# A depthwise convolution in a two-block transformer: seven of its 31 taps on ScalarE with accumulating DMAs, and its layer norm's statistics summed before their matmuls

## The chip, the cores and the metric

One core of one Trainium2 chip. The time is the device time of one execution in microseconds, and less is better. 256 tokens of width 2048 go through two transformer blocks; about 500 MB of fp32 weights are read once from HBM.

## What is computed

Block one: attention of three branches beside a conformer convolution, then an output projection and a feed-forward layer; block two is another transformer block. The change touches only the convolution branch of block one:

```python
def conformer_conv(h2, conv_w, conv_b, ln_g, ln_b):
    a, gate = jnp.split(h2, 2, axis=-1)
    u = a * jax.nn.sigmoid(gate)
    u = causal_depthwise_conv(u, conv_w, conv_b)     # 31 taps, 1024 channels, 256 tokens
    u = layer_norm(u, ln_g, ln_b)                    # over the 1024 channels
    return jax.nn.silu(u)
...
    attn = nsa_attention(q, kv, gates, ...)
    conv = conformer_conv(conv_in, ...)
    x = x + jnp.concatenate([attn, conv], axis=-1) @ w_out
```

Tap k multiplies the channel's tokens by one weight and adds them, shifted by s = 30 - k tokens. The layer norm takes mean and variance of each token over all 1024 channels.

## The kernel before

**Weights.** They come as items of 512 KB (`raw`, four buffers, loaded by SP's queue). `split_upto` (line 272) makes of each a rounded copy `hi` on ScalarE (line 281) and the rest `lo` on VectorE (line 282), with four buffers of each, three items ahead of the one that TensorE works on. `run_items` (line 288) does an item in two halves of six products `acc` of 512 columns (`hi` and `lo` with the high part of the activations, `hi` with the low part), twelve in all, and calls `pump` (line 242) after each half.

**Order.** The groups of block one run as `ORDER` says: convolution input quarters c0, c1, c2, the gates g, q0, the compressed branch cmp, c3, the windowed and selected branches' keys win and slc, q1, then the output projection: oc (convolution rows), oa and ob. Everything that isn't weights stands in pipes, lists of closures; `pump` takes steps from them at the rates of `RATES`. Within an engine instructions run in the order in which they were issued.

**The convolution.** Channels lie on the partitions, tokens in the free dimension; a quarter q is two tiles of 128 channels x 256 tokens, kept as one 128x512 tile. `conv_in(q)` (line 493) makes `u` from two projections and puts 31 steps into the pipe `conv`, one for each tap. `conv_tap` (line 517) does both halves of a tap: the first tap (k = 30) on ScalarE with the bias (line 523), the other 30 on VectorE, one multiply-add each into `y` (line 526), 240 in all. After the fourth quarter `conv_norm` (line 529) follows in the same pipe: `mean` multiplies each of the eight tiles by a constant matrix `avg` (8 matmuls), `center` subtracts the mean on VectorE (line 539) and squares on ScalarE (`sqc`, line 541), `var` does 16 matmuls of one column, `rs` and `rs2` make the reciprocal root (`lnv`, `lnd`, `lnr`), and `scale`, `silu` and `low` make `th`, `sh` and `sl`, the activations of the group oc. That group can't start before them; its item asks the pipe for each tile (`mixT`).

**Attention beside it.** The same stretch of the program holds the scores `s`, maxima (line 796) and exponentials (line 802) of the attention pipe, and the copies `kx` (lines 738 and 739) of the transposed keys. POOL issues the loads of bias rows M from a DRAM table gsc, which is itself written by four DMAs of 768 KB from POOL, the small weights w1 and w, and lq.

Of the kernel before, what the change touches and what calls it, by code (L numbers as in the profile page):

```python
# [19 lines left out]
AF = mybir.ActivationFunctionType  # L20
# [16 lines left out]
NRAW = 4  # L37
LN_DVE = 0
ORDER = ["c0", "c1", "c2", "g", "q0", "cmp", "c3", "win", "slc", "q1", "oc", "oa", "ob"]
RATES = {"c1": {"conv": 1}, "win": {"attn": 0.25}, "q1": {"attn": 0.34, "conv": 1.5},  # L40
         "oc": {"attn": 0.5, "conv": 2}, "oa": {"attn": 1}}


# [80 lines left out]
def body(tc, A, out, stop=None, dbg=None):  # L124
# [26 lines left out]
    def U(s="u", dt=F32):  # L151
        return big.tile([P, 512], dt, name=nm(s), tag="U", bufs=NU)

    def two(t):
        return t.rearrange("p (a b) -> p a b", a=2)
# [4 lines left out]
    def bank(s="bg"):  # L160
        return psB.tile([P, 512], F32, name=nm(s), tag="bg")

    def mm(o, l, r, start=False, stop=False):
        pe.matmul(o, l, r, start=start, stop=stop, skip_group_check=True)  # L164
# [171 lines left out]
    def col(name, i):  # L336
        c = offs[name] + i
        return cols[:, c:c + 1]
# [147 lines left out]
    w_in = w2d("w_in")  # L486


    us, ys = {}, {}
    conv, attn = Pipe(), Pipe()  # L490
    mixT = Acts(lambda kt: conv if kt >= 8 else attn)

    def conv_in(q):

        def post(acc):
            s, u = U("sig"), U("ut")
            uu = [two(u)[:, 0], two(u)[:, 1]]
            for t in range(2):
                act.activation(two(s)[:, t], acc[t][:, :T], AF.Sigmoid, scale=rstd[:, t:t + 1])
                dve.scalar_tensor_tensor(uu[t], acc[t][:, T:], rstd[:, t:t + 1], two(s)[:, t],  # L500
                                         op0=ALU.mult, op1=ALU.mult)

            def f():
                us[q], ys[q] = U("u"), U("y")
                turn_plain(us[q], uu, 0)
                for k in range(30, -1, -1):
                    conv.push(lambda k=k: conv_tap(q, k))
                if q == 3:
                    conv_norm()
            urgent.push(None)  # L510
            urgent.push(f)
        return post

    def conv_group(q):
        group(w_in, None, 512, allk, xT, conv_in(q), parts=[(3632 + q * T, T), (2608 + q * T, T)])

    def conv_tap(q, k):
        u2, y2 = two(us[q]), two(ys[q])
        for kk in range(2):
            f = 2 * q + kk  # L520
            w = col("conv_w", k * 8 + f)
            if k == 30:
                act.activation(y2[:, kk], u2[:, kk], AF.Identity, scale=w, bias=col("conv_b", f))
            else:
                s = 30 - k
                dve.scalar_tensor_tensor(y2[:, kk, s:], u2[:, kk, :T - s], w, y2[:, kk, s:],  # L526
                                         op0=ALU.mult, op1=ALU.add)

    def conv_norm():
        st = {}  # L530

        def mean():
            b = st["m"] = bank("mean")
            for f in range(8):
                mm(b[:, :T], avg, two(ys[f // 2])[:, f % 2], start=f == 0, stop=f == 7)

        def center(q):
            mb = st["m"][:, :T].unsqueeze(1).broadcast_to([P, 2, T])
            dve.tensor_tensor(two(ys[q]), two(ys[q]), mb, op=ALU.subtract)
            s = st[q] = U("sqc")  # L540
            act.activation(s, ys[q], AF.Square)

        def var():

            b = st["v"] = bank("var")
            for t in range(2):
                for f in range(8):
                    mm(b[:, t:t + 1], two(st[f // 2])[:, f % 2, t * P:(t + 1) * P], avg[:, 0:1],
                       start=f == t == 0, stop=f == 7)

        half_gb = keep.tile([P, 16], F32, name="half_gb")

        def rs():
            c = offs["conv_ln_g"]
            dve.tensor_scalar(half_gb, cols[:, c:c + 16], 0.5, None, op0=ALU.mult)
            v = small("lnv")
            dve.tensor_scalar(v[:, :2], st.pop("v")[:, :2], EPS, None, op0=ALU.add)
            newton_rstd(v[:, 2:4], v[:, :2], 2)
            d = st["d"] = U("lnd")
            for t in range(2):  # L560
                dve.tensor_scalar(d[:, t * P:(t + 1) * P], ident, v[:, 2 + t:3 + t], 1024.0,
                                  op0=ALU.mult, op1=ALU.mult)

        def rs2():

            b = bank("lnr")
            mm(b[:, :T], avg, st.pop("d")[:, :T], start=True, stop=True)
            r = U("lnr")
            act.copy(r[:, :T], b[:, :T])
            st["r"] = r[:, :T]  # L570

        def scale(q, kk):
            y = two(ys[q])[:, kk]
            dve.tensor_tensor(y, y, st["r"], op=ALU.mult)

            if kk == 0:
                st[q] = U("th")
            f = 2 * q + kk
            g, b = half_gb[:, f:f + 1], half_gb[:, 8 + f:9 + f]
            act.activation(two(st[q])[:, kk], y, AF.Tanh, scale=g, bias=b)  # L580
            if LN_DVE:
                dve.tensor_scalar(y, y, g, b, op0=ALU.mult, op1=ALU.add)
            else:
                act.activation(y, y, AF.Identity, scale=g, bias=b)

        def silu(q):
            y = ys[q]
            dve.scalar_tensor_tensor(y, st.pop(q), 1.0, y, op0=ALU.add, op1=ALU.mult)
            hi = st["hi", q] = U("sh", F32R)
            act.copy(hi, y)  # L590

        def low(q):
            hi, lo = st["hi", q], U("sl", F32R)
            dve.tensor_tensor(lo, ys[q], hi.bitcast(F32), op=ALU.subtract)  # L594
            for kk in range(2):
                mixT.put(8 + 2 * q + kk, two(hi)[:, kk], two(lo)[:, kk])

        for f in (mean, None):
            conv.push(f)
        for q in range(4):  # L600
            conv.push(lambda q=q: center(q))
        for f in (None, var, rs, None, rs2):
            conv.push(f)
        for q in range(4):
            conv.push(lambda q=q: scale(q, 0))
            conv.push(lambda q=q: scale(q, 1), None, lambda q=q: silu(q), None, lambda q=q: low(q))
# [40 lines left out]
    def post_cmp(acc):  # L647
# [24 lines left out]
        def hidden(i):  # L672
            def f():
                b = st[("b", i)] = bank("hid")
                o = b[0:64, :60]
                for lp in range(16):
                    e_, m = divmod(lp, 8)
                    xv = st[i][e_].rearrange("p (h n b) -> p h n b", h=4, b=8)
                    w = w1t[i][e_].rearrange("p (l c) -> p l c", l=8)[:, m]
                    mm(o, w, xv[:, :, e_:e_ + 15, m], start=lp == 0, stop=lp == 15)  # L680
            return f

        def silu():
# [921 lines left out]
```

## Time and profile before

| | us |
|---|---|
| median of 3 runs (lowest, highest) | 2830.05 (2829.97, 2831.06) |
| the profiled execution | 2829.45 |
| its span in the trace | 2827.5 |
| TensorE busy | 2793.4 |
| VectorE busy | 1631.5 |
| ScalarE busy | 1423.6 |

The mean granted clock of TensorE is 0.996 of full speed. The chain of work that ended last lies on TensorE for 96% of the span. A busy time is that of the profiled execution alone; the time of an execution is a little longer than the span of its instructions.

### The profile page before, as it was taken

The numbers are of one execution on the slowest core, as the hardware profiler recorded it, in microseconds if no ns is written. First come the engines' busy times: TensorE is split into PE (matmuls) and PEld (weight loads), VectorE is DVE, ScalarE is ACT, GpSimd is POOL, SyncE is SP. The second block draws the span as 40 slices with busy tenths as digits, with TensorE's granted clock in tenths as the row PEclk, the third lists the DMA queues.
The fourth block names the chain that finished last, engine by engine and source line by source line (L and its number), as shares of the span: only waits on it lengthen the run. The fifth ranks groups of instructions, "written<-read, shape, count | busy, mean of one in ns | idle before, by whom it ended". The sixth has DMA issues, their size and how long they took to land.

```text
span 2827.5 us, 34906 instructions
## 1 busy us (share of the span) xinstructions
PE 2793.4 (99%) x13031; PEld 2314.5 (82%) x13031; DVE 1631.5 (58%) x2472; ACT 1423.6 (50%) x2072; POOL 36.6 (1%) x73
## 2 busy tenths in 40 slices
PE   8998999999999999999999999999999999999998
PEld 7886778888888888889888888888888888888887
DVE  6887765656666554565554545555555455454444
ACT  5456565555555444566544555554454444444443
POOL 1200000000000000000000000000000000000000
PEclk9999999999999999999999999999999999999999
DMA  7853345666556666654566555665566666666664
GB/s 232 236 165 119 116 136 184 187 186 186 180 180 195 198 197 193 179 173 129 170 197 193 172 165 173 179 197 187 183 189 187 192 187 192 187 187 196 197 197 160
DMA packets 279579, 513.01 MB, mean 181 GB/s; under 512 B 21223, under 2 KB 46739, under 8 KB 279409
## 3 DMA queue, kind: packets, MB, share of 16 engines
q1 hardware_dynamic: 272256, 502.86, 58.4%
q0 software_dynamic: 4624, 7.13, 0.9%
q8 instruction: 102, 1.67, 0.2%
q10 hardware_dynamic: 2528, 0.79, 0.1%
q14 instruction: 69, 0.56, 0.1%
HBM read 505.45 MB, written 5.24 MB: 181 GB/s over the span
## 4 chain that ended last, share of the span: by engine, by line
PE 96%; DVE 1%; ACT 1%; issue 1%; DMA 0%; SPq 0%; DVEq 0%; ACTq 0%
PE acc L164 90%; PE tr L391 2%; PE ms L164 1%; PE o L164 0%; DMA raw<-in_w_in 0%; PE ds L164 0%; PE mo L164 0%; PE do L164 0%; DVE lo L282 0%; ACT hi L281 0%; ACT p L802 0%; PE hid L164 0%; PE s L164 0%; PE pt L807 0%; DVE y L526 0%
## 5 line engine op out<-in xcount | busy, mean ns | idle before, releaser
L282 DVE TENSOR_TENSOR lo<-raw,hi 128x1024 fp32r<-128x1024 f32 (+3 forms) x956 | 1153.3, 1211 | 1013.7 <-ACT hi L281 993.1
L281 ACT CAST hi<-raw 128x1024 fp32r<-128x1024 f32 (+3 forms) x956 | 989.8, 1040 | 879.3 <-PE acc L164 821.2
L164 PE MATMUL acc<-hi,xh 128*128 128x512 f32 (+2 forms) x3200 | 1261.2, 394 | 2.8 <-ACT xh L405 2.8
L164 PE MATMUL acc<-hi,xl 128*128 128x512 f32 (+2 forms) x3200 | 1241.8, 388 | 0.5 <-DVE xl L407 0.5
L164 PE MATMUL acc<-lo,xh 128*128 128x512 f32 (+2 forms) x3200 | 1240.0, 388 | 0.0
L164 PEld LDWEIGHTS acc<-hi,xl 128*128 128x128 f32 x3200 | 601.7, 188 | 123.7 <-DVE xl L407 1.0
L164 PEld LDWEIGHTS acc<-hi,xh 128*128 128x128 f32 x3200 | 602.2, 188 | 118.4 <-ACT xh L405 3.0
L164 PEld LDWEIGHTS acc<-lo,xh 128*128 128x128 f32 x3200 | 602.8, 188 | 115.9 <-DVE lo L282 0.5
L164 PE MATMUL acc<-hi,sh 128*128 128x512 f32 x480 | 192.1, 400 | 10.7 <-ACT sh L590 10.7
L164 PE MATMUL acc<-hi,sl 128*128 128x512 f32 x480 | 187.7, 391 | 0.0
L164 PE MATMUL acc<-lo,sh 128*128 128x512 f32 x480 | 187.6, 391 | 0.0
L164 PEld LDWEIGHTS acc<-hi,sh 128*128 128x128 f32 x480 | 90.6, 189 | 29.4 <-ACT sh L590 11.1
L164 PEld LDWEIGHTS acc<-hi,sl 128*128 128x128 f32 x480 | 90.5, 188 | 19.6 <-DVE sl L594 0.2
L164 PEld LDWEIGHTS acc<-lo,sh 128*128 128x128 f32 x480 | 90.7, 189 | 17.6
L526 DVE SCALAR_TENSOR_TENSOR y<-u,cols,y 128x255 f32<-128x255 f32 (+14 forms) x240 | 96.3, 464 | 0.0
L1043 DVE SCALAR_TENSOR_TENSOR yf<-tr,cols,yf 128x254 f32<-128x254 f32 (+1 forms) x176 | 72.6, 475 | 29.3 <-ACT yf L1038 29.3
L1038 ACT ACTIVATE yf<-tr,cols 128x256 f32<-128x256 f32 x88 | 44.8, 560 | 33.7 <-PE tr L391 33.7
L164 PE MATMUL acc<-hi,ymh 128*128 128x512 f32 x128 | 49.8, 389 | 0.0
L164 PE MATMUL acc<-lo,ymh 128*128 128x512 f32 x128 | 49.8, 389 | 0.0
L164 PE MATMUL acc<-hi,yml 128*128 128x512 f32 x128 | 49.8, 389 | 0.0
L428 ACT ACTIVATE e<-acc,rstd 128x512 f32<-128x512 f32 x54 | 37.0, 690 | 25.2 <-PE acc L164 25.2
L434 ACT ACTIVATE junk<-xs 128x512 f32<-128x512 f32 x48 | 30.0, 629 | 35.8 <-DVE xs L442 14.3
(314 smaller groups left out, 1373.5 us busy)
## 6 DMA issues: line engine op xcount, KB each, us to landing
raw<-in_w_in SPq DMA_DIRECT2D x216, 512.0 KB, 3.7
raw<-in_w_up SPq DMA_DIRECT2D x176, 512.0 KB, 3.8
raw<-in_w_down SPq DMA_DIRECT2D x88, 512.0 KB, 4.4
raw<-in_w_ffn_gate SPq DMA_DIRECT2D x88, 512.0 KB, 4.3
raw<-in_w_ffn_up SPq DMA_DIRECT2D x88, 512.0 KB, 3.8
raw<-in_w_ffn_down SPq DMA_DIRECT2D x88, 512.0 KB, 4.3
raw<-in_w_out SPq DMA_DIRECT2D x64, 512.0 KB, 3.7
raw<-in_w_in SPq DMA_DIRECT2D x64, 256.0 KB, 3.4
```

Source lines behind the costliest of these rows:

```text
L164: pe.matmul(o, l, r, start=start, stop=stop, skip_group_check=True)
L281: act.copy(it.hi[:, c], it.raw[:, c])
L282: dve.tensor_tensor(it.lo[:, c], it.raw[:, c], it.hi[:, c].bitcast(F32), op=ALU.subtract)
L391: pe.transpose(b[:, kk * T + t * P: kk * T + (t + 1) * P], src[t][:, c:c + P], ident)
L428: act.activation(u[:, :n], acc[t][:, :n], AF.Copy, scale=scale[:, t:t + 1])
L434: act.activation(j[:, :n], src, AF.Square, accum_out=acc)
L526: dve.scalar_tensor_tensor(y2[:, kk, s:], u2[:, kk, :T - s], w, y2[:, kk, s:], op0=ALU.mult, op1=ALU.add)
L1038: act.activation(y2[:, kk], t2[:, kk], AF.Identity, scale=c(2), bias=col("ffn_conv_b", f))
L1043: dve.scalar_tensor_tensor(y2[:, kk, s:], t2[:, kk, :T - s], col("ffn_conv_w", k * 88 + f), y2[:, kk, s:], op0=ALU.mult, op1=ALU.add)
```

## The change

Of the 31 taps of a quarter, the seven with shift s = 3, 7, 11, 15, 19, 23 and 27 leave VectorE. `conv_product` multiplies on ScalarE: for s = 3 straight into a new tile `z` (POOL clears its first three columns), for the six others into a tile `pr`, which one step of the pipe later a DMA from POOL's software queue adds to `z` (`conv_gather`, 24 in all, some 250 KB each). A gather waits for its product and for the gather before it, both on `z`. After the last tap `conv_join` adds `z` to `y`, and `conv_sum` adds the quarters up in `csum`. `mean` then takes 2 matmuls; the centers stand two to a step, their squares are summed on VectorE one after another, and `var` takes 4 matmuls. The pipe's rate in the group c1 goes from 1 to 0.85, and the compressed branch's `hidden` takes three more steps of the pipe at each of its calls.

```diff
-RATES = {"c1": {"conv": 1}, ...
+RATES = {"c1": {"conv": 0.85}, ...
...
                 for k in range(30, -1, -1):
-                    conv.push(lambda k=k: conv_tap(q, k))
+                    if (30 - k) % 4 == 3:
+                        continue
+                    if (29 - k) % 4 == 1 and k > 1:
+                        conv.push(lambda k=k: (conv_tap(q, k), conv_product(q, k - 1)),
+                                  lambda k=k: conv_gather(q, k - 1))
+                    else:
+                        conv.push(lambda k=k: conv_tap(q, k))
+                conv.push(lambda: conv_join(q))
+                if q:
+                    conv.push(lambda: conv_sum(q))
...
+    def conv_product(q, k):
+        s = 30 - k
+        if s == 3:
+            z = zs[q]
+            pool_e.memset(two(z)[:, :, :s], 0.0)
+        else:
+            z = prods[q, k] = U("pr")
+        for kk in range(2):
+            act.activation(two(z)[:, kk, s:], two(us[q])[:, kk, :T - s], AF.Copy,
+                           scale=col("conv_w", k * 8 + 2 * q + kk))
+
+    def conv_gather(q, k):
+        s = 30 - k
+        if s > 3:
+            pool_e.dma_start(two(zs[q])[:, :, s:], two(prods.pop((q, k)))[:, :, s:],
+                             accum_op=ALU.add)
+
+    def conv_join(q):
+        dve.tensor_tensor(ys[q], ys[q], zs[q], op=ALU.add)
+
+    def conv_sum(q):
+        if q == 1:
+            csum.append(U("csum"))
+        s = csum[0]
+        dve.tensor_tensor(s, ys[q], s if q > 1 else ys[0], op=ALU.add)
...
         def mean():
-            for f in range(8):
-                mm(b[:, :T], avg, two(ys[f // 2])[:, f % 2], start=f == 0, stop=f == 7)
+            s = two(csum.pop())
+            for kk in range(2):
+                mm(b[:, :T], avg, s[:, kk], start=kk == 0, stop=kk == 1)
...
             act.activation(s, ys[q], AF.Square)
+            if q:
+                p = st[q - 1]
+                dve.tensor_tensor(s, s, p, op=ALU.add)
...
         def var():
+            s = two(st[3])
             for t in range(2):
-                for f in range(8):
-                    mm(b[:, t:t + 1], two(st[f // 2])[:, f % 2, t * P:(t + 1) * P], avg[:, 0:1],
-                       start=f == t == 0, stop=f == 7)
+                for kk in range(2):
+                    mm(b[:, t:t + 1], s[:, kk, t * P:(t + 1) * P], avg[:, 0:1],
+                       start=kk == t == 0, stop=kk == 1)
...
-        for q in range(4):
-            conv.push(lambda q=q: center(q))
+        for q in (0, 2):
+            conv.push(lambda q=q: (center(q), center(q + 1)))
...
+                for _ in range(3):
+                    conv.step()
```

**Where the mean stands on TensorE.** Rows are an instruction's line, operation, out<-in and size; a number behind a name tells one tile from another. Before, the mean (one row for each quarter) stands behind the second head group's scores, in the middle of q1:

```order
L164 MATMUL s_2181<-kx_89,q_1168 128x271
L164 MATMUL s_2182<-kx_89,q_1168 128x271
L164 MATMUL s_2181<-kx_89,q_1168 128x143
L164 MATMUL s_2182<-kx_89,q_1168 128x143
L164 MATMUL mean_2203<-y_509,avg 128x256 x2
L164 MATMUL mean_2203<-y_715,avg 128x256 x2
L164 MATMUL mean_2203<-y_929,avg 128x256 x2
L164 MATMUL mean_2203<-y_1671,avg 128x256 x2
L164 MATMUL acc_2023<-hi_2052,xh_278 128x512
L164 MATMUL acc_2023<-lo_2053,xh_278 128x512
```

In the change it stands ahead of the transposes of the keys `kt` that the first scores need:

```order
L164 MATMUL acc_2110<-lo_2030,xh_128 128x512
L164 MATMUL acc_2110<-hi_2029,xl_129 128x512
L164 MATMUL mean_2125<-csum_1333,avg 128x256 x2
L391 MATMUL tr_2128<-ident,kt_2098 128x128 x4
L164 MATMUL acc_2109<-hi_2049,xh_187 128x512
L164 MATMUL acc_2109<-lo_2050,xh_187 128x512
L164 MATMUL acc_2109<-hi_2049,xl_188 128x512
L164 MATMUL acc_2110<-hi_2049,xh_187 128x512
```

So it moved forward past 42 products, two sets of scores and the transposes, and what stands behind it now includes all of these.

**What VectorE does between mean and var.** Before, the four centers stand apart, with an item's `lo` and the gate operations between them:

```order
L539 TENSOR_TENSOR y_509<-y_509,mean_2203 128x512
L282 TENSOR_TENSOR lo_2222<-raw_2056,hi_2221 128x1024
L539 TENSOR_TENSOR y_715<-y_715,mean_2203 128x512
L850 RECIPROCAL rg_2254<-sm_2185 128x4
L853 TENSOR_TENSOR rg_2254<-rg_2254,gates 128x2
L855 TENSOR_SCALAR p_2183<-p_2183,rg_2254 128x256
L856 TENSOR_SCALAR p_2183<-p_2183,rg_2254 128x128
L853 TENSOR_TENSOR rg_2254<-rg_2254,gates 128x2
L855 TENSOR_SCALAR p_2184<-p_2184,rg_2254 128x256
L856 TENSOR_SCALAR p_2184<-p_2184,rg_2254 128x128
L861 TENSOR_TENSOR pc_2068<-pc_2068,cmx_2069 128x8x15
L539 TENSOR_TENSOR y_929<-y_929,mean_2203 128x512
```

In the change they stand behind the first maxima, in one run with the additions of squares (line 585), each of which needs ScalarE's square of the center before it:

```order
L844 ISA cmx_2154 128x1
L580 TENSOR_TENSOR y_509<-y_509,mean_2125 128x512
L580 TENSOR_TENSOR y_725<-y_725,mean_2125 128x512
L585 TENSOR_TENSOR sqc_2188<-sqc_2188,sqc_2185 128x512
L580 TENSOR_TENSOR y_947<-y_947,mean_2125 128x512
L585 TENSOR_TENSOR sqc_2192<-sqc_2192,sqc_2188 128x512
L580 TENSOR_TENSOR y_1737<-y_1737,mean_2125 128x512
L585 TENSOR_TENSOR sqc_2196<-sqc_2196,sqc_2192 128x512
L282 TENSOR_TENSOR lo_2200<-raw_2053,hi_2199 128x1024
L993 SCALAR_TENSOR_TENSOR lj_2205,le_2206<-lq_1958 128x128 x2
```

The `lo` of the next item (line 282) and the lambda operations (line 993) moved behind the whole run.

**What POOL issues ahead of the last join.** Before, gsc's last write, the loads lq and the first M stand together, early in the program:

```order
L711 MEMSET vcmp_1605 128x512
L711 MEMSET vcmp_1611 128x512
L778 DMA gsc<-gm 512x1x384
L356 DMA lq_1880<-in_lambda_q_2 128x128
L356 DMA lq_1880<-in_lambda_k_2 128x128
...
L791 DMA M_2064<-gsc 128x2x256
L791 DMA M_2066<-gsc 128x2x256
L823 MEMSET pc_2068 128x256
L791 DMA M_2571<-gsc 128x2x256
```

In the change gathers (line 542) stand among them; here those of the first quarter (`z_510`) about gsc's first write, and the last four of the fourth (`z_1738`):

```order
L532 MEMSET z_510 128x2x3
L542 DMA z_510<-pr_613 128x2x249
L542 DMA z_510<-pr_658 128x2x245
L826 DMA gsc<-gm 512x1x384
L542 DMA z_510<-pr_712 128x2x241
...
L542 DMA z_1738<-pr_1915 128x2x241
L356 DMA lq_1958<-in_lambda_q_2 128x128
L356 DMA lq_1958<-in_lambda_k_2 128x128
...
L542 DMA z_1738<-pr_1977 128x2x237
L542 DMA z_1738<-pr_2017 128x2x233
L542 DMA z_1738<-pr_2063 128x2x229
L839 DMA M_2149<-gsc 128x2x256
```

gsc's first write now stands between the second and the third gather of the first quarter; the lq loads moved between the third and the fourth gather of the last, the M loads behind its last.

## Rows read from the trace of the kernel before

**Rows 1.** The page's first part (busy time and share of the span of each engine) and the head of its fourth (the chain that ended last, by engine).

```profile
...
PE 2793.4 (99%) x13031; PEld 2314.5 (82%) x13031; DVE 1631.5 (58%) x2472; ACT 1423.6 (50%) x2072; POOL 36.6 (1%) x73
...
PE 96%; DVE 1%; ACT 1%; issue 1%; DMA 0%; SPq 0%; DVEq 0%; ACTq 0%
...
```

**Rows 2.** Windows: the stretch in us, its length, then for each engine the busy time in it and (x) its instructions: TensorE, its weight loads, VectorE, ScalarE, POOL; then the granted TensorE clock as a share of full speed, the DMA engines' busy share, GB/s.

```profile
...
200.00:220.00 20.00, 20.00 (x95) 16.21 (x94) 19.91 (x38) 10.95 (x16) 0.00 (x0) 1.00 0.71 207
220.00:240.00 20.00, 16.89 (x72) 13.31 (x71) 17.90 (x71) 8.72 (x23) 1.75 (x3) 0.91 0.42 132
240.00:260.00 20.00, 11.41 (x73) 9.53 (x71) 11.59 (x37) 15.08 (x29) 2.26 (x4) 0.88 0.33 103
260.00:280.00 20.00, 17.92 (x94) 13.58 (x94) 13.68 (x40) 15.42 (x32) 1.82 (x3) 0.86 0.26 77
400.00:2827.00 2427.00, 2418.38 (x11142) 2016.74 (x11140) 1322.02 (x1693) 1197.35 (x1627) 4.92 (x16) 1.00 0.60 184
...
```

**Rows 3.** TensorE's waits over the whole span: the waiting instruction, what it waited for, us in all, times, the longest.

```profile
...
PE acc L164 <- ACT sh L590: 10.7, 1, 10.7
...
PE mean L164 <- DVE y L526: 3.1, 1, 3.1
...
```

**Rows 4.** TensorE's timeline: start, time taken, line, operation, out<-in, how many records; in brackets the idle time before and what ended it.

```profile
...
212.05 0.39 PE L164 MATMUL acc<-lo,xh 128*128 128x512 f32 x1
212.28 0.39 PE L164 MATMUL acc<-hi,xl 128*128 128x512 f32 x1
...
215.23 0.60 PE L391 MATMUL tr<-ident,kt 128*128 128x128 f32 x4
...
227.34 2.86 PE L164 MATMUL mean<-y,avg 128*128 128x256 f32 x12
233.30 1.13 PE L164 MATMUL mean<-y,avg 128*128 128x256 f32 x4 [3.11 <-DVE y L526]
...
243.41 3.62 PE L164 MATMUL var<-avg,sqc 128*128 128x1 f32 x32
...
250.82 0.59 PE L164 MATMUL lnr<-lnd,avg 128*128 128x256 f32 x2
262.08 0.79 PE L164 MATMUL acc<-hi,sh 128*128 128x512 f32 x1 [10.67 <-ACT sh L590]
...
263.10 0.63 PE L164 MATMUL acc<-hi,sl 128*128 128x512 f32 x1
263.53 0.63 PE L164 MATMUL acc<-hi,sh 128*128 128x512 f32 x1
...
268.13 0.60 PE L391 MATMUL tr<-ident,e 128*128 128x128 f32 x4
...
```

**Rows 5.** Windows of 5 us, columns as in rows 2.

```profile
...
230.00:235.00 5.00, 1.89 (x8) 1.49 (x8) 5.00 (x10) 0.00 (x0) 0.72 (x1) 0.98 0.32 105
235.00:240.00 5.00, 5.00 (x17) 3.87 (x17) 3.34 (x19) 3.32 (x10) 0.31 (x1) 0.68 0.55 159
260.00:265.00 5.00, 2.92 (x7) 2.29 (x8) 2.80 (x7) 4.90 (x10) 0.00 (x0) 0.50 0.13 48
...
```

**Rows 6.** The page's group of the VectorE taps (count, busy us, mean ns of one, idle before), and the instructions of line 523 with least, median and greatest duration in ns.

```profile
...
L526 DVE SCALAR_TENSOR_TENSOR y<-u,cols,y 128x255 f32<-128x255 f32 (+14 forms) x240 | 96.3, 464 | 0.0
...
L523 ACT ACTIVATE y<-u,cols x8: 587/592/601, 46.3 to 186.5; 128x256 f32<-128x256 f32 x8
...
```

**Rows 7.** VectorE's timeline, columns as in rows 4.

```profile
...
214.18 1.59 DVE L526 SCALAR_TENSOR_TENSOR y<-u,cols,y 128x239 f32<-128x239 f32 x4
215.69 1.22 DVE L282 TENSOR_TENSOR lo<-raw,hi 128x1024 fp32r<-128x1024 f32 x1
...
220.38 0.42 DVE L796 CUSTOM_DVE_ANT_0 p<-s,M 128x256 f32<-128x256 f32 x1
...
221.85 2.32 DVE L526 SCALAR_TENSOR_TENSOR y<-u,cols,y 128x234 f32<-128x234 f32 x6
...
236.13 0.69 DVE L539 TENSOR_TENSOR y<-y,mean 128x512 f32<-128x512 f32 x1
...
```

**Rows 8.** ScalarE's timeline, columns as in rows 4.

```profile
207.26 1.05 ACT L281 CAST hi<-raw 128x1024 fp32r<-128x1024 f32 x1 [1.66 <-PE acc L164]
209.98 1.06 ACT L281 CAST hi<-raw 128x1024 fp32r<-128x1024 f32 x1 [1.67 <-PE acc L164]
...
213.47 1.06 ACT L281 CAST hi<-raw 128x1024 fp32r<-128x1024 f32 x1
215.87 0.58 ACT L738 COPY kx<-tr 64x512 f32<-64x512 f32 x1 [1.33 <-PE tr L391]
...
242.76 1.23 ACT L541 ACTIVATE sqc<-y 128x512 f32<-128x512 f32 x2
...
```

**Rows 9.** DMA issues in four stretches, 60 to 74, 86 to 95, 230 to 240 and 264 to 272 us: out<-in, the issuing queue, how many, KB each, median us from issue to landing.

```profile
...
gsc<-gm POOLq DMA_DIRECT2D x1, 768.0 KB, 12.2
...
M<-gsc POOLq DMA_DIRECT2D x2, 256.0 KB, 14.9
...
M<-gsc POOLq DMA_DIRECT2D x1, 256.0 KB, 4.2
...
M<-gsc POOLq DMA_DIRECT2D x2, 256.0 KB, 3.4
...
```

**Rows 10.** POOL's timeline, columns as in rows 4.

```profile
...
234.14 0.72 POOL L791 DMA_DIRECT2D M<-gsc  x1 [7.26 <-issue]
...
```

More of the change, by code (lines that the diff above doesn't have):

```diff
@@ L39 @@
 ORDER = ["c0", "c1", "c2", "g", "q0", "cmp", "c3", "win", "slc", "q1", "oc", "oa", "ob"]
-RATES = {"c1": {"conv": 1}, "win": {"attn": 0.25}, "q1": {"attn": 0.34, "conv": 1.5},
+RATES = {"c1": {"conv": 0.85}, "win": {"attn": 0.25}, "q1": {"attn": 0.34, "conv": 1.5},
          "oc": {"attn": 0.5, "conv": 2}, "oa": {"attn": 1}}
@@ L486, in body @@
     w_in = w2d("w_in")
-    us, ys = {}, {}
+    us, ys, zs, prods = {}, {}, {}, {}
     conv, attn = Pipe(), Pipe()
@@ L503, in f @@
             def f():
-                us[q], ys[q] = U("u"), U("y")
+                us[q], ys[q], zs[q] = U("u"), U("y"), U("z")
                 turn_plain(us[q], uu, 0)
                 for k in range(30, -1, -1):
-                    conv.push(lambda k=k: conv_tap(q, k))
+                    if (30 - k) % 4 == 3:
[8 more added lines that the diff above has]
+                    conv.push(lambda: conv_sum(q))
                 if q == 3:
@@ L527, in conv_tap @@
                                          op0=ALU.mult, op1=ALU.add)
+    csum = []
+    def conv_sum(q):
[3 more added lines that the diff above has]
+        dve.tensor_tensor(s, ys[q], s if q > 1 else ys[0], op=ALU.add)
     def conv_norm():
```

## The prediction

> **What bounds the kernel now.** I read the page first: TensorE is busy 99% of the span and carries 96% of the chain that ended last, so only time in which TensorE stands still or runs slowly can be won [rows 1]. Then the busy time by 20 us: the reader sees 20.00 of 20 at a clock of 1.00 up to 220 us, then 16.89, 11.41 and 17.92, and after 400 us 2418 of 2427 [rows 2]. All that this change touches lies before 270 us. TensorE's waits name two in that stretch: 10.7 us for the first `sh` of the output projection, 3.1 us for the last tap of the convolution [rows 3]. TensorE's timeline places them: the mean's twelve records at 227.34 and, after the wait, four at 233.30; var's 32 at 243.41; nothing between `lnr` at 250.82 and 262.08 [rows 4]. After both waits the clock falls to its lower level, 1.2 GHz: 0.68 on average in 235 to 240, 0.50 in 260 to 265 [rows 5]; products then start 0.43 us apart, not 0.23 [rows 4], which costs 1.8 us after the first wait and 1.6 after the second (8 to 9 products each). Lost from 212 to 268: 3.1 + 10.7 + 1.8 + 1.6 = **17.2 us**.
>
> **TensorE's own saving.** mean goes from 8 matmuls to 2, var from 16 to 4. Mean's records take 2.86 + 1.13 = 4.0 us, of which three quarters go: 3.0. Var's take 3.6; 2.7 go [rows 4]. Together 5.7 us. With the 17.2 the most that could be won is 22.9 us, if nothing new were waited for.
>
> **Seven taps leave VectorE.** 56 of the 240 taps [rows 6], some 0.375 us each from start to start (four in 1.59, [rows 7]), are 21 us less there; four joins, three sums and three additions of squares at about 0.65 (a 128x512 tensor operation takes 0.69, [rows 7]) put 6.5 back. ScalarE gets 56 products. The nearest row is the first tap, already a ScalarE product from SBUF: 592 ns [rows 6], so some 0.55 us each, 31 us spread over 170. Before 212 us neither is on TensorE's path: TensorE is full there [rows 2], and ScalarE's next copy `hi` waits 1.67 us of each 2.72 us for TensorE to free a buffer [rows 8]; one or two products fit in that. Cost and gain: 0. If that cover is gone, the products show as a late `hi`, at most 1.1 us per item.
>
> **Six gathers per quarter.** Each is a software-queue DMA of about 250 KB that adds `pr` to `z`; it waits for its product and for the gather before it, and POOL waits in order, so M, gsc, w1 and lq loads are queued behind it and it behind them. No row shows an accumulating DMA. The nearest are POOL's 256 KB copies of M: 3.4 and 4.2 us from issue to landing, 14.9 right behind the 768 KB gsc [rows 9]. An accumulation reads its target too, so I bound L, issue to landing, by 3.4 below and by 7 (twice the bare copy) above, and take **4.4**, just above the copy. The Trainium skill ("DMA: Bandwidth & Descriptors", Anatomy of one DMA) gives 2.0 us plus bytes over 436 GB/s, an estimate of 2.6; the copies here are slower, and the sum would be the same by it.
>
> The last quarter decides. Its products stand behind the copies `hi` of the items in order, at about 184, 189.4, 192.2, 197.7, 203.1 and 208.9 (the last behind the `hi` of 207.26, [rows 8]). With L = 5.25 the gathers land at 189.3, 194.7, 199.9, 205.2, 210.4 and 215.7; the join can start, as shown next, at 215.7. So up to 5.25 nothing is late. In the first quarter the third gather stands behind gsc, whose landing takes 12.2 [rows 9]; it is about 8 us late there, and the weights' lookahead of three items (3 x 2.72) covers that at 4.4.
>
> **The chain from 212 to 268.** Here `hi` of q1's fourth lookahead item runs at 213.47 [rows 8]; its `lo` no longer stands behind taps and ends at 215.7 (before: it started at 215.69). Join and sum, 2 x 0.65: `mean` starts at 217.0. It now stands on TensorE ahead of the transposes that were done at 215.23 [rows 4]: a new wait of 1.8 us, and transposes, four copies `kx` (0.6 each), `hi`, `lo` and the maxima (1.47, from 220.38 to 221.85, [rows 7]) all follow it: maxima end at 224.7, before at 221.85.
>
> Then two engines hand over in turn. VectorE: center 0, 1, add, center 2, add, center 3, add; ScalarE: a square after each center, 0.6 [rows 8]. Center 0 ends 225.4, square 1 at 226.7, add 1 at 227.4, center 2 at 228.0, its square 228.6, add 229.3, center 3 at 229.9, square 230.5, add **231.15**. TensorE is at `var` at 225.0: a new wait of 6.2 us. Next `hi`, `lo` (232.6), the lambda and gate operations (235.3), variance to `lnd` 2.0 us as before (247.07 to 249.0): `lnr` at about 238, against 250.82.
>
> So the statistics come 13 us earlier. But the work between them and the transposes of `e` is the same as before, and before it was done while TensorE stood still: ScalarE was busy 15.1 and 15.4 of 20 us in those slices [rows 2]. In order on ScalarE now: `hi`, maxima and four exponentials to 245.1, three tanh pairs (1.12 each) to 248.5, `sh` 249.0, `hi` 250.1 and `lo` 251.2 of oc0, `sl` of the second tile 254.2 (TensorE waits 2.5), `hi` and `lo` of oc1 to 259, the two other `sh`, `hi` and `lo` of oc2 to 265.1, exponentials 267.3, the two `e` at **268.5**. The transposes of `e` then start at 268.6; before, at 268.13 [rows 4]. TensorE stands still some 10 us just ahead of them.
>
> Check by TensorE: 52.9 us before (215.23 to 268.13), less 17.2 and 5.7, is 30; new waits 1.8 + 6.2 + 0.8 + 2.5 + 10 = 21.3; half-clock products between them 2. Sum 53.3, as above.
>
> **Sum.** +0.5 us at the transposes of `e`, and the lower clock after the 10 us wait, 1.6, which before fell ahead of that point: **+2 us**. The profiled execution took 2829.45 (span 2827.5); with the change 2831.5. The median of the runs is 0.6 above it: **2832**. Some forty steps of the chain are added by hand; I give it 4 us to either side, 2828 to 2836. A measurement here tells 0.2%, 5.7 us, from no change: 2824.3 to 2835.7.
>
> **Rivals.** *A, slower: the gathers become the chain.* It decides from L = 5.25 on. At 6 us the last quarter lands at 220.0, 4.3 us late, at 7 at 226, 10.3 late, and all of the chain above moves with it. The first two quarters, with gsc and the w1 loads in the same queue, add up to as much again, since their 8 us of lookahead are used up: 2836 to 2841 at 6, 2842 to 2853 at 7; I price it at **2843**. For it: the 14.9 us behind gsc, a DMA share of 0.71 in 200 to 220 [rows 2] where the M copies saw less. Against: no M copy that stood alone took over 4.2. The Trainium skill ("DMA: Bandwidth & Descriptors", Queues, rings and completion order) has descriptors of one ring start in order, and the 14.9 agrees.
>
> *B, slower: POOL cannot issue beside VectorE.* VectorE is busy 19.91 of 20 us in 200 to 220 [rows 2]; if an issue waited for it, L would grow by a `lo` or a run of taps, 1.2 to 2.3 us, to about 6.2: **2839** by A's steps. Against it: POOL issued M in 0.72 us at 234.14 [rows 10], in a stretch of 5 us in which VectorE was busy all 5.00 [rows 5]. The Trainium skill ("SBUF — State Buffer", SBUF: two separate sides) says that a POOL-issued DMA starves while VectorE runs in a two-port mode, 620 ns growing to 3100; no row here shows it.
>
> *C, faster: the hand-over is shorter than I booked.* From 217 to 268.5 are 51 us, of which ScalarE is busy 36 by my steps; 15 are waits for VectorE. If two thirds of them fall away because operations run beside each other that I put in line, the transposes of `e` come 10 us earlier: **2822**; if all do, 2817; the cap of 22.9 off the median of before gives 2807. A third, 2827, is still the forecast. For it: the statistics are ready 13 us earlier and TensorE has 21 us of slack. Against: both engines work in program order, and every step above waits for the one before.
>
> **How the numbers follow.** Forecast 0.50, A 0.27, B 0.04, C 0.19. Of the forecast 0.04 lie above 2835.7, and of C 0.01 above 2824.3: faster 0.18, same 0.47, slower 0.35. The range leaves out half of C (below 2822) and the part of A with L over 6.5 (above 2848).
>
> **What would show it.** The wait for taps gone, TensorE idle 1 to 3 us ahead of `mean` at about 217, 5 to 8 ahead of `var`, 8 to 11 ahead of the transposes of `e` near 268.6, and mean and var of some 1 us each; gathers landing in under 5.25 us. Wrong, if the gathers take over 5.25 and the join of the last quarter starts after 216, or if the transposes of `e` start before 263 with TensorE hardly waiting.

## The result and the profile after

| | before | with the change |
|---|---|---|
| median of 4 runs, us | 2830.01 | 2854.25 (2852.15 to 2858.40) |
| the profiled execution, us | 2829.45 | 2855.76 |
| its span, us | 2827.5 | 2853.9 |

The change is slower: ratio 1.0086, 95% interval 1.0074 to 1.0098, some 24 us, above the range of 2822 to 2848. The forecast said no change; of its rivals the one that came about is A, the gathers as the chain, and it cost more than priced.

The page of the change, answering to [rows 1]:

```profile
...
PE 2801.0 (98%) x12995; PEld 2316.6 (81%) x12995; DVE 1617.9 (57%) x2426; ACT 1444.5 (51%) x2128; POOL 65.6 (2%) x101
...
PE acc L164 84%; PE tr L391 2%; DMA z<-pr 2%; DMA raw<-in_w_in 1%; PE ms L164 1%; DVE lo L282 1%; ACT hi L281 1%; PE o L164 0%; ACT p L850 0%; PE ds L164 0%; PE mo L164 0%; PE do L164 0%; PE s L164 0%; PE pt L855 0%; PE pt L856 0%
...
```

VectorE lost only 13.6 us of its busy time, ScalarE gained 21, and in the chain a term stands that was not there before: the landing of gathers, 2% of the span by itself. TensorE's waits, against [rows 3]:

```profile
...
PE mean L164 <- DVE csum L567: 9.6, 1, 9.6
PE tr L391 <- ACT e L428: 5.4, 3, 3.8
PE var L164 <- DVE sqc L585: 4.9, 1, 4.9
PE pt L855 <- DVE mx L844: 4.5, 1, 4.5
PE tr L391 <- DVE ut L500: 3.9, 1, 3.9
PE s L164 <- ACT pts L858: 3.5, 1, 3.5
...
```

The 10.7 us for `sh` and the 3.1 for the last tap are gone, as forecast. But the wait ahead of `mean` is 9.6 us, not 1.8, and TensorE now loses time early in the program too. Two of its early windows in the kernel before, columns as in [rows 2]:

```profile
...
100.00:120.00 20.00, 20.00 (x94) 16.57 (x93) 17.20 (x32) 9.28 (x11) 0.00 (x0) 1.00 0.74 218
180.00:200.00 20.00, 20.00 (x92) 16.57 (x91) 19.43 (x38) 12.44 (x18) 0.00 (x0) 1.00 0.69 191
...
```

The same two, and 220 to 240, with the change:

```profile
...
100.00:120.00 20.00, 15.69 (x66) 11.85 (x64) 13.87 (x26) 7.43 (x11) 6.23 (x8) 1.00 0.88 245
180.00:200.00 20.00, 16.10 (x62) 12.73 (x61) 13.98 (x23) 14.29 (x25) 2.93 (x5) 0.83 0.72 205
220.00:240.00 20.00, 10.37 (x44) 8.29 (x43) 10.38 (x18) 5.39 (x10) 4.21 (x5) 0.86 0.77 226
...
```

TensorE loses 4.3 us in 100 to 120 and 3.9 in 180 to 200, where it was full before, and half of 220 to 240, where it lost 3.1 before [rows 2]. VectorE's timeline (start and length in us, line, operation, and in brackets the idle time before it with its releaser) tells of the first and the third place:

```profile
...
86.04 0.81 DVE L557 SCALAR_TENSOR_TENSOR y<-u,cols,y 128x226 f32<-128x226 f32 x2
93.20 0.69 DVE L546 TENSOR_TENSOR y<-y,z 128x512 f32<-128x512 f32 x1 [6.34 <-POOL z L532]
...
237.38 0.69 DVE L546 TENSOR_TENSOR y<-y,z 128x512 f32<-128x512 f32 x1 [7.37 <-DMA z<-pr]
238.11 0.69 DVE L567 TENSOR_TENSOR csum<-y,csum 128x512 f32<-128x512 f32 x1
```

The join of the first quarter keeps VectorE idle for 6.3 us (the bracket names an older event of `z`; the sixth gather was issued at 89.20 and landed at 93.1), that of the last for 7.4. The way from the first join to TensorE leads through a weight load: `lo` of item 30 stands behind it and runs at 93.81 (88.87 before), so the buffer that it frees is loaded at 95.06 and not at 90.11, and ScalarE's `hi` at 105.52 waits 7.75 us for these weights. POOL's timeline, in the same columns, shows why they are late:

```profile
...
60.88 1.62 POOL L826 DMA_DIRECT2D gsc<-gm  x1
66.08 1.20 POOL L542 DMA_DIRECT2D z<-pr  x1 [3.58 <-ACT pr L536]
77.47 1.18 POOL L542 DMA_DIRECT2D z<-pr  x1 [10.19 <-ACT pr L536]
...
168.62 1.18 POOL L542 DMA_DIRECT2D z<-pr  x1 [3.75 <-DMA z<-pr]
169.32 1.00 POOL L735 MEMSET hidv<- 64x512 f32 x1
...
213.67 1.24 POOL L542 DMA_DIRECT2D z<-pr  x1 [0.95 <-issue]
222.79 1.21 POOL L542 DMA_DIRECT2D z<-pr  x1 [7.88 <-DMA z<-pr]
229.23 1.20 POOL L542 DMA_DIRECT2D z<-pr  x1 [5.23 <-DVE y L557]
...
```

The third gather (66.08) stands behind gsc's first write and lands 10.9 us later; the fourth is issued 0.5 us after that (the bracket at 77.47 names the product, which had long been made). So it is nearly everywhere: of the 20 gathers that follow another one of their quarter, 19 are issued 0.5 to 0.6 us after its landing. The fourth of the last quarter (213.67), behind the lq loads, lands after 8.5 us, and POOL waits 7.88 us for it. The landings, in the columns of [rows 9], first of 60 to 80 us, then of 200 to 215:

```profile
...
gsc<-gm POOLq DMA_DIRECT2D x1, 768.0 KB, 13.5
z<-pr POOLq DMA_DIRECT2D x1, 245.0 KB, 5.3
z<-pr POOLq DMA_DIRECT2D x1, 241.0 KB, 10.9
z<-pr POOLq DMA_DIRECT2D x1, 237.0 KB, 5.2
...
z<-pr POOLq DMA_DIRECT2D x1, 241.0 KB, 3.8
z<-pr POOLq DMA_DIRECT2D x1, 237.0 KB, 8.5
lq<-in_lambda_q POOLq DMA_DIRECT2D x2, 64.0 KB, 6.2
...
```

And ScalarE's timeline shows the second place, which no step of the prediction had:

```profile
...
161.16 0.21 ACT L733 ACTIVATE hidk<-hid 64x60 f32<-64x60 f32 x1
170.36 0.53 ACT L739 ACTIVATE hidv<-hid 64x60 f32<-64x60 f32 x4 [8.98 <-POOL hidv L735]
...
180.12 2.13 ACT L763 COPY vcmp<-vc 32x128 f32<-32x128 f32 x8 [4.72 <-POOL vcmp L759]
...
```

The compressed branch's tiles hidv and vcmp are cleared by memsets on POOL. At 169.32 the memset of hidv stands behind a gather that waited for the landing of the one before (POOL's rows above), and ScalarE, with every later `hi` behind it, waits 8.98 and then 4.72 us.

Where the time went is read best from the copy `hi` of each item (counted from 0): its start against the same item's in the kernel before (ScalarE's timelines, us). The labels are those of the experiments below.

| item | before, start | change | e3 | e8 | e12 | e9 | e10 |
|---|---|---|---|---|---|---|---|
| 31 | 91.15 | -1.0 | +0.2 | -1.5 | -0.1 | -1.2 | -1.7 |
| 41 | 120.11 | +7.1 | +0.2 | -1.1 | -0.1 | -1.2 | +7.9 |
| 61 | 185.03 | +13.8 | +0.2 | +9.9 | -0.1 | -1.2 | +15.8 |
| 71 | 213.47 | +13.8 | +0.2 | +9.9 | +3.7 | -0.4 | +13.3 |
| 83 | 283.23 | +26.2 | +3.3 | +22.4 | +16.4 | +11.9 | +16.7 |

(The -1 to -1.7 of the early items is in place before the first gather.) The change loses in three steps: 8.1 us behind the first join, 6.7 about the memsets, 12.3 from the last join on. After the 83rd item nothing more is lost.

### The profile page after: what moved, and what is told of

Same layout as the page of the kernel before. It is cut to its first block, busy times and chain, and to the rows that moved or that the text cites. A ratio compares the mean times of both kernels' runs of the same rounds, so it can differ in the third digit from the quotient of the medians.

```text
span 2853.9 us, 34913 instructions
## 1 busy us (share of the span) xinstructions
PE 2801.0 (98%) x12995; PEld 2316.6 (81%) x12995; DVE 1617.9 (57%) x2426; ACT 1444.5 (51%) x2128; POOL 65.6 (2%) x101
## 4 chain that ended last, share of the span: by engine, by line
PE 89%; DMA 3%; ACT 2%; DVE 2%; issue 1%; POOL 0%; DVEq 0%; SPq 0%; ACTq 0%; POOLq 0%
PE acc L164 84%; PE tr L391 2%; DMA z<-pr 2%; DMA raw<-in_w_in 1%; PE ms L164 1%; DVE lo L282 1%; ACT hi L281 1%; PE o L164 0%; ACT p L850 0%; PE ds L164 0%; PE mo L164 0%; PE do L164 0%; PE s L164 0%; PE pt L855 0%; PE pt L856 0%
## 5 line engine op out<-in xcount | busy, mean ns | idle before, releaser
L557 DVE SCALAR_TENSOR_TENSOR y<-u,cols,y 128x255 f32<-128x255 f32 (+22 forms) x184 | 74.3, 464 | 0.0
```

## The experiments

Theory Q: the gathers, in POOL's queue, cost nearly all of it. Rival S: the statistics' serial chain of center, square and addition does. Each ratio is against runs of the kernel before that were made beside it.

**e3, no gathers.** The edit, in `conv_gather`:

```diff
-            pool_e.dma_start(two(zs[q])[:, :, s:], two(prods.pop((q, k)))[:, :, s:],
-                             accum_op=ALU.add)
+            prods.pop((q, k))
```

> The change without its 24 accumulating DMAs: the products of six of the seven taps are made on ScalarE and left out of the sum; all else stays. Theory Q: 2829 to 2834, the forecast's 2832 with nothing late in the queue: mean at about 217, var's wait some 6 us. Rival S: 2845 or more, unchanged by the DMAs. A third case, ScalarE's products themselves delay hi: over 2836 with ScalarE's hi late by 0.5 us or more in 60 to 210.

Measured 2832.52, ratio 1.0008 (0.9999 to 1.0018): the forecast's number. TensorE's timeline in the stretch that the prediction worked out by hand:

```profile
...
217.36 1.13 PE L164 MATMUL mean<-csum,avg 128*128 128x256 f32 x4 [1.79 <-DVE csum L566]
...
231.71 1.64 PE L164 MATMUL var<-avg,sqc 128*128 128x1 f32 x8 [5.05 <-DVE sqc L584]
...
238.47 0.74 PE L164 MATMUL lnr<-lnd,avg 128*128 128x256 f32 x2
...
254.72 0.92 PE L164 MATMUL s<-kd,q 64*128 64x256 f32 x6 [3.49 <-ACT pts L857]
...
267.36 0.48 PE L854 MATMUL pt<-ident,p 128*128 128x128 f32 x1 [4.51 <-DVE mx L843]
...
269.62 1.47 PE L391 MATMUL tr<-ident,e 128*128 128x128 f32 x4 [1.35 <-ACT e L428]
...
```

`mean` at 217.4 after a wait of 1.79 (forecast 217.0 and 1.8), var at 231.7 after 5.05 (231.2 and 6.2), `lnr` at 238.5 (238), the transposes of `e` at 269.6 (268.6), with 3.49, 4.51 and 1.35 us idle ahead of them in three waits (10). So the gathers cost 22 us and everything else in the change 2.5. As the cause of the 22 us S falls, and so does the third case: ScalarE's products hold back no `hi` for long (items 49 and 50, at 144 and 145, are 0.4 and 0.9 us late, item 51 is 0.2 again).

**e1, sums only.** All taps on VectorE as before, no products, c1's rate 1, no extra steps; csum, paired centers and the sums of squares stay:

```diff
-                    if (29 - k) % 4 == 1 and k > 1:
-                        conv.push(lambda k=k: (conv_tap(q, k), conv_product(q, k - 1)),
-                                  lambda k=k: conv_gather(q, k - 1))
...
-                conv.push(lambda: conv_join(q))
+                    conv.push(lambda k=k: conv_tap(q, k))
```

> Only the sums of the change: all taps as before, no product on ScalarE, no DMA; csum, paired centers, squares summed on VectorE, 2 + 4 matmuls. Theory Q (the gathers in POOL's queue cost nearly all of the 24 us): no loss of that size here, between 2828 and 2838; the taps last as long as before, so the wait ahead of mean stays and the serial centers follow it. Rival S (the statistics' serial chain of center, square and addition costs it): 2845 or more, with the waits ahead of var and of the first sh longer by over 10 us.

Measured 2841.65, ratio 1.0039 (1.0024 to 1.0053): between the two cases, 3.7 above Q's range. So the sums are not free by themselves. TensorE's timeline:

```profile
...
238.67 2.05 PE L164 MATMUL mean<-csum,avg 128*128 128x256 f32 x4 [8.18 <-DVE csum L559]
...
251.37 1.86 PE L164 MATMUL var<-avg,sqc 128*128 128x1 f32 x8 [5.39 <-DVE sqc L577]
...
263.02 1.22 PE L164 MATMUL lnr<-lnd,avg 128*128 128x256 f32 x2 [3.31 <-DVE lnd L598]
273.55 0.80 PE L164 MATMUL acc<-hi,sh 128*128 128x512 f32 x1 [9.30 <-ACT sh L627]
...
```

The taps are as long as before, but two of the three sums stand in the pipe ahead of the last taps: VectorE does two of these (four instructions) at 236.26, behind an item's `lo` and the second maxima, where before all were done ahead of both, at 233.6. The last sum follows. So `mean` waits 8.2 us (3.1 before) and starts at 238.7, and the serial squares and the scaling follow 20 to 25 us later than in e3. The sums cost 12 us where the taps end late, and nothing that e3 shows where they end early.

**e2, products and gathers only.** mean, center and var as in the kernel before; all else as in the change:

```diff
-            s = two(csum.pop())
-            for kk in range(2):
-                mm(b[:, :T], avg, s[:, kk], start=kk == 0, stop=kk == 1)
+            for f in range(8):
+                mm(b[:, :T], avg, two(ys[f // 2])[:, f % 2], start=f == 0, stop=f == 7)
```

> Products and gathers as in the change, mean and var as before (8 and 16 matmuls, single centers, no additions). Theory Q: 2848 to 2856, since the gathers stay; join of the last quarter as late as in the change. Rival S: 2832 to 2838.

Measured 2854.24, ratio 1.0082 (1.0067 to 1.0097): as Q says. With the gathers in, the form of the statistics makes no difference that these runs can tell.

**e6, plain copies.** The accumulation is taken out of the DMA:

```diff
-            pool_e.dma_start(two(zs[q])[:, :, s:], two(prods.pop((q, k)))[:, :, s:],
-                             accum_op=ALU.add)
+            pool_e.dma_start(two(zs[q])[:, :, s:], two(prods.pop((q, k)))[:, :, s:])
```

> The change with its gathers as plain copies, without the accumulation (six of the seven products overwrite one another in z, so they are left out of the sum); every wait and the queue stay. If the accumulation itself makes the landing long: copies of about 250 KB land in 3.4 to 4.2 us as M's did, and the time falls to 2836 to 2846. If queue and company make it (theory Q as I now hold it): alone 3.5 to 5 us, still 8 to 11 beside gsc, w1 and lq, and 2848 to 2855.

Measured 2835.10, ratio 1.0014 (1.0005 to 1.0024), a little under the first case; the ten runs lie between 2832.24 and 2837.34, and the trace is of one of 2832.28. All instructions and waits are those of the change; only the accumulation is gone, and with it 19 us. So theory Q in the form that it then had (queue and company make the landing long, whatever is moved) missed: it needs the accumulation. The group of the gathers' issues in the change (shortest, median and longest in ns, then the first and the last start):

```profile
...
L542 POOL DMA_DIRECT2D z<-pr x24: 1165/1188/1289, 54.2 to 229.2; - x24
...
```

The same group in e6:

```profile
...
L542 POOL DMA_DIRECT2D z<-pr x24: 711/714/738, 54.0 to 210.6; - x24
...
```

And the landings (last column, median us), in the change:

```profile
...
z<-pr POOLq DMA_DIRECT2D x4, 249.0 KB, 6.5
...
z<-pr POOLq DMA_DIRECT2D x4, 233.0 KB, 5.5
...
```

and of the same two sizes in e6:

```profile
...
z<-pr POOLq DMA_DIRECT2D x4, 249.0 KB, 4.7
...
z<-pr POOLq DMA_DIRECT2D x4, 233.0 KB, 3.2
...
```

The record of an issue is 1.19 us long with the accumulation and 0.71 without; but POOL isn't held up longer, since its next instruction starts 0.7 us after the issue in both (168.62 to 169.32 in POOL's rows above; 81.73 to 82.43 in e6). What differs is the landing, 5.5 to 6.5 us against 3.2 to 4.7 in these rows. That doesn't look like 19 us; but the six of a quarter are in series. In the change 18 of the 24 land after 3.7 to 5.9 us, 4.7 in the median; in e6 20 land after 2.5 to 5.0, 4.2 in the median. The next issue comes some 0.55 us later in both: a period of 5.2 us against 4.7, where the prediction's schedule allows 5.25. The others, beside gsc, w1, lq and M, land after 7.5 to 11.0 us (six) and 5.5 to 8.0 (four). The change stood at the point where the chain keeps up, with nothing left for the late ones.

**e7, two chains.** Two tiles `z`, used in turn; shifts 3 and 7 go straight into them, 20 gathers remain, two joins:

```diff
-        if s == 3:
-            z = zs[q]
+        if s in (3, 7):
+            z = zs[q][s == 7]
...
-            pool_e.dma_start(two(zs[q])[:, :, s:], ...
+            pool_e.dma_start(two(zs[q][(s // 4) % 2])[:, :, s:], ...
```

> Two tiles z, taken in turn: shifts 3 and 7 go straight into them, the five gathers of a quarter alternate, so a gather waits for the landing of the one before the last, and 20 gathers remain; the join becomes two additions. Theory Q: POOL no longer stands still for a landing, the gathers behind gsc, w1 and lq overlap, and most of the 22 us go: 2833 to 2842, with DMA waits ahead of the joins under 3 us in all. Rival: the bandwidth of the queue is the limit rather than the wait for each landing; then 2848 to 2856.

Measured 2834.70, ratio 1.0013 (1.0004 to 1.0022). VectorE's waits, in the columns of [rows 3], have one for a landing ahead of a join, where the change had three, of 16.5 us in all:

```profile
...
DVE y L547 <- DMA z<-pr: 0.4, 1, 0.4
...
```

Of the 12 gathers that follow another one into their tile three are issued 0.5 us after its landing (78.43, 81.14 and 153.80), the others over a microsecond after it. They land no sooner (5.6 to 7.3 us in the medians by shift); it is the wait of each for the one before that costs, not the queue's bandwidth. That each quarter also has one gather less may be a part of it; no run has a single chain of five.

**e5, additions on POOL; e11, additions on VectorE.** In place of the DMA:

```diff
+            z = two(zs[q])[:, :, s:]
+            pool_e.tensor_tensor(z, z, two(prods.pop((q, k)))[:, :, s:], op=ALU.add)    # e5
+            dve.tensor_tensor(z, z, two(prods.pop((q, k)))[:, :, s:], op=ALU.add)       # e11
```

> The change with each of the 24 accumulating DMAs replaced by an addition z += pr on POOL itself (tensor_tensor, 128 x 2 x 249 and less): same products, same order on POOL, no transfer to land. Theory Q (the landing of the gathers, 3.7 to 5.6 us alone and 8 to 11 in company, is the chain): an addition under 4 us cannot be late in any quarter, so 2831 to 2836, as without gathers (2832.5). Rival: POOL and VectorE hold one another up; then the taps on VectorE grow above 0.46 us or the additions above 5 us, and the time is 2840 or more.

> The change with each gather replaced by an addition z += pr on VectorE: nothing stands in POOL's queue, VectorE takes 24 x 0.6 = 14 us of its 21 back. Theory Q: 2832 to 2838, the taps of the last quarter ending some 3 us later than without gathers. Rival (VectorE's load of these quarters matters as much as the queue): 2840 or more.

e5: 2844.10, ratio 1.0045 (1.0030 to 1.0060), 8 us above Q's range; e11: 2834.35, ratio 1.0014 (1.0005 to 1.0024), within it. In e5 an addition takes 1.65 us (the middle of the three numbers) and 3.47 at most, so none is late by itself, as the group of POOL's additions shows:

```profile
...
L543 POOL TENSOR_TENSOR z<-z,pr x24: 1215/1645/3468, 54.6 to 216.4; 128x498 f32<-128x498 f32 x4, 128x490 f32<-128x490 f32 x4, 128x482 f32<-128x482 f32 x4, 128x474 f32<-128x474 f32 x4
...
```

What it loses instead it loses on VectorE, as the rival said. The group of the taps in e3 and then in e5, in the columns of [rows 6]:

```profile
...
L556 DVE SCALAR_TENSOR_TENSOR y<-u,cols,y 128x255 f32<-128x255 f32 (+22 forms) x184 | 74.1, 462 | 0.0
...
L557 DVE SCALAR_TENSOR_TENSOR y<-u,cols,y 128x255 f32<-128x255 f32 (+22 forms) x184 | 96.3, 580 | 0.0
...
```

Beside the additions the same 184 taps take 22 us more; 23 of them take over 0.6 us, the median (0.46) doesn't show it. It costs 7.5 us at one place: `lo` of item 42 runs at 126.45 (122.29 in e6), so the weights of item 46 are loaded at 127.69, 1.9 us behind gsc's third write (125.84), and ScalarE's `hi` at 140.60 waits 8.36 us for them. In e6 the same load goes out at 123.55, 3.3 us ahead of the write, and is in time. The last quarter costs 5 us more than in e3 (`mean` waits 4.6 us). e11 puts 24 additions of 0.65 us, 16 us, back on VectorE and costs 2 us over e3.

**e9 and e10, where.** Gathers in the last quarter alone, and in the first three alone:

```diff
-        if s > 3:
+        if s > 3 and q == 3:    # e9
+        if s > 3 and q < 3:     # e10
```

> The change with gathers in the last quarter alone (six DMAs); the products of the other quarters are made and left out of the sum. If the losses add up by place: without gathers 2832.5, and the last quarter's own 9 us (its copies hi fell back 12.3 us in the change, 3.3 without gathers) give 2839 to 2844. If the last quarter is late only because the earlier ones are: 2832 to 2836.

> The complement: gathers in the first three quarters alone (18 DMAs), the last quarter's six products left out of the sum. If the losses add up by place: 2832.5 plus the 8 us up to the 41st item and the 6.7 between the 50th and the 60th, 2845 to 2849. If they are the same backlog, carried to the end: 2836 to 2843.

e9: 2842.39, ratio 1.0044 (1.0027 to 1.0061); e10: 2846.51, ratio 1.0055 (1.0040 to 1.0070). Over e3's 2832.5 that is 9.9 and 14.0; together 2856.4, against the change's 2854.3. Within 2 us, the runs' own spread, the losses add up by place. In the first three quarters there is more than in the last, on which the prediction had put its weight.

**e4, e8 and e12, the first three quarters.** e4 puts the memsets on VectorE:

```diff
-            pool_e.memset(hv[0:64], 0.0)
+            dve.memset(hv[0:64], 0.0)
...
-                pool_e.memset(v, 0.0)
+                dve.memset(v, 0.0)
```

e8 leaves them and moves the joins of the first three quarters ten taps into the next one:

```diff
+                    if q and k == 20:
+                        conv.push(lambda: conv_join(q - 1))
+                        if q > 1:
+                            conv.push(lambda: conv_sum(q - 1))
...
-                conv.push(lambda: conv_join(q))
-                if q:
-                    conv.push(lambda: conv_sum(q))
                 if q == 3:
+                    conv.push(lambda: conv_join(q))
+                    conv.push(lambda: conv_sum(q))
```

e12 is e8 with the memsets still on POOL, but issued ahead of the compressed branch's matmuls (hidv's at 139.4, in e8 at 165.9):

```diff
+                if i == 0:
+                    st["hv"], st["vc"] = U("hidv"), [U("vcmp"), U("vcmp")]
+                    pool_e.memset(st["hv"][0:64], 0.0)
+                    for v in st["vc"]:
+                        pool_e.memset(v, 0.0)
                 av = two(turn4(e, i * T))
```

> The change with the memsets of hidv and vcmp on VectorE rather than on POOL, where they stand behind gathers. In the trace of the change ScalarE waits 9.0 and 4.7 us for them near 170 and 180, and the copies hi fall back by 6.7 us between the 50th and the 60th item. Theory Q, POOL's order part: those two waits go and the time falls by 4 to 7 us, to 2847 to 2850. Rival (the waits are covered, the loss there is the gathers' own chain): less than 2 us.

> The change with the joins of the first three quarters ten taps into the next quarter, rather than right behind the last tap; the last quarter's stays. In the trace of the change VectorE stands 6.3 us ahead of the first join, the copies hi then fall back 8 us between the 31st and the 41st item. Theory Q: those 7 to 8 us go and the last quarter's 9 to 12 stay: 2842 to 2849. Rival (the loss at the 31st to 41st item comes from the weight loads beside gsc and w1, not from the join): 2851 to 2856.

> Late joins (as in the run with late joins alone) and the memsets of hidv and vcmp issued on POOL ahead of the compressed branch's matmuls, so that no gather stands before them; all gathers stay. With late joins alone the copies hi fell back 10 us between the 51st and the 60th item and ScalarE waited 12.1 and 4.9 us for the two memsets. If POOL's order makes that loss: those waits go, and what is left is the last quarter's 9.9 us over 2832.5, so 2840 to 2846. If the gathers' own chain makes it: 2850 to 2856, with VectorE waiting for the landing ahead of the late joins.

e4: 2855.56, ratio 1.0093 (1.0076 to 1.0110); e8: 2855.09, ratio 1.0087 (1.0070 to 1.0104); e12: 2847.01, ratio 1.0063 (1.0046 to 1.0080). By their times e4 and e8 do nothing, as the rivals said. The table tells otherwise for e8: the 8 us up to the 41st item are gone, and between the 51st and the 60th 10 come back. Ten taps later VectorE stands at no join, but the next quarter's first gather now falls right behind gsc's third write (issued at 138.09, 1.2 us behind the write, landed after 17.2 us), the rest of that quarter queue behind it, and ScalarE waits 12.1 us for the memset. In e4 the memset only changed its queue: on VectorE it stands behind the taps that the extra pipe steps bunch up, as VectorE's timeline of e4 shows:

```profile
...
161.38 3.87 DVE L557 SCALAR_TENSOR_TENSOR y<-u,cols,y 128x242 f32<-128x242 f32 x10
...
166.31 0.83 DVE L557 SCALAR_TENSOR_TENSOR y<-u,cols,y 128x235 f32<-128x235 f32 x2
167.19 0.48 DVE L735 MEMSET hidv<- 64x512 f32 x1
```

There ScalarE waits 6.0 and 5.0 us for VectorE. Only e12 takes away both, and then the 61st item is where it was before (table); its ScalarE timeline shows no wait where there were 8.98 us:

```profile
...
155.31 0.21 ACT L740 ACTIVATE hidk<-hid 64x60 f32<-64x60 f32 x1
155.43 0.52 ACT L745 ACTIVATE hidv<-hid 64x60 f32<-64x60 f32 x4
```

Left is the last quarter, 12.7 us from the 71st to the 83rd item (3.1 without gathers), and 3.8 just before, where the first gather again falls behind gsc; so e12 ends 1 us above what was expected. In the first three quarters taking one loss away (e8) let the next one grow in its place, and only both edits together (e12) show what each is worth.

## Why the prediction was wrong

- **The step that failed** is the one that took L = 4.4 us for every gather and said "up to 5.25 nothing is late", and that the first quarter's lookahead covers its gather behind gsc. Measured in the change, 18 of the 24 land in 3.7 to 5.9 us, 4.7 in the median, and the next is issued 0.5 us after the landing (66.08 + 10.9 = 77.0, issue 77.47), which the chain of the prediction left out: some 5.2 in all, the limit itself. The other six, beside gsc, w1, lq and M, take 7.5 to 11 us, beyond its upper bound of 7, two of them in the quarter that was to decide. The prediction had the 12.2 and the 14.9 of [rows 9] and booked such company for one gather of the first quarter only; the three items of lookahead that were to cover it did not, as 8.1 us were lost behind the first join.
- **Rival A** had the mechanism and its point of decision (5.25), but it priced "the first two quarters" at "as much again" as the last and the third at nothing. The first three cost 14.0 us (e10), the last 9.9 (e9). Missing was a consumer: the list of what stands behind a waiting POOL named loads and not the two memsets, for which ScalarE waits.
- **The chain from 212 to 268**, forecast at +2 us, was measured without gathers at +2.5 (e3), its milestones within 1.1 us. That two engines handing over in turn give back what the statistics gain was right. That some forty steps added by hand came out within a microsecond is in part luck: the waits ahead of `e` came as three (3.49, 4.51 and 1.35), not as one of 10 behind one of 2.5.
- **TensorE's own saving** came: four records of mean and eight of var in place of 16 and 32. It is worth nothing here, since TensorE waits for the engines that feed it.
- **VectorE and ScalarE before 212 us**: right; in e3 `hi` is 0.2 us late at items 41, 61 and 71, though ScalarE's products were booked at 31 us and its busy time grew by 21. (TensorE was not quite full "up to 220": it was busy 11.77 us of the first 20 and 19.61 of 80 to 100, to no effect on the sum.)
- **Rival B** (POOL cannot issue beside VectorE) is not it: POOL's next instruction starts 0.7 us after a gather, as after a copy beside the same VectorE (e6). **Rival C** (shorter hand-over): no, by e3.

## What to carry to other kernels

Work that is moved to a queue in series must be priced by its period, landing plus re-issue, in the company that it will have, and compared with the spacing of its producer; here 5.2 us against the 5.25 of the schedule left nothing for the six late landings. Then list everything behind the waiting engine, small memsets too, since another engine may wait for one of them. Two independent accumulators took nearly all of the loss away (e7, with one gather less per quarter); moving the consumer alone did not (e8). And a gain on one engine is worth nothing while two others, in program order, set the pace of the stretch: without any gather the change would still have been no faster.

## What the runs showed of the hardware

- An accumulating DMA of some 240 KB within SBUF landed after 3.7 to 5.9 us in 18 of 24 cases (the change), a plain copy of the same pieces after 2.5 to 5.0 in 20 of 24 (e6); the rest stood beside gsc, w1, lq or M. The Trainium skill ("DMA: Bandwidth & Descriptors", Anatomy of one DMA) has a formula by which this size would take an estimated 2.6 us; the accumulations and the copies' medians lie above it, and the measurement decides.
- The record of its issue is 1.19 us long, not 0.71, but POOL's next instruction starts 0.7 us after it all the same. Records right behind it grow too: loads of M 1.22 us for 0.71 and the memset of hidv 1.00 for 0.54 (the change and e6).
- Behind a 768 KB write in the same queue a gather landed after 10.9, 17.2 and 17.8 us (the change at 66.08, e8 at 138.09, e12 at 138.60), each time 2.6 to 2.8 us after the write itself had landed.
- An addition of 128x458 to 128x498 on POOL takes 1.2 to 3.5 us, and beside 24 of them the taps on VectorE took 580 ns in the mean, not 462, the longest 1.53 us, not 0.48 (e5 against e3 and the change), the median staying at 0.46. The Trainium skill ("SBUF — State Buffer", Who interferes with whom) lets an operation with two SBUF inputs on VectorE and a POOL operation that reads SBUF block one another; the longest tap and the mean agree.
